# Gated DeltaNet layer: solving for the writes times the keys' reciprocal norms

## The chip, the cores and the metric

The kernel runs on one core of one Trainium2 chip. The time is the device time of one execution in microseconds (us); of several runs the median is given. A core has TensorE (PE, with its weight loads shown apart as PEld), VectorE (DVE), ScalarE (ACT), GpSimd (POOL) and SyncE (SP), which issues the DMAs of this kernel. Each engine works through its own queue in order and waits on semaphores that other engines raise.

## The reference

Two layers work on 1040 tokens (16 learned ones and 1024 given ones) of width 1024. Layer A is a gated DeltaNet with 8 heads of width 128; layer B is a latent attention that the change does not touch. Of layer A, what matters is this:

```python
k = l2_norm(k)                       # per token and head: k * rsqrt(sum(k*k) + EPS)
beta = sigmoid(b_raw)
g = -exp(a_log) * softplus(a_raw + dt_bias)
# per chunk, with gc = cumsum(g):
decay = exp(gc_i - gc_j) for j <= i
lower = strict_tril((k * beta) @ k.T * decay)
(I + lower) u = beta * v - (beta * k * exp(gc)) @ S      # solved for the writes u
o = (q * exp(gc)) @ S + tril(q @ k.T * decay) @ u
S = S * exp(gc_last) + (k * exp(gc_last - gc)).T @ u
```

The kernel works with chunks of 128 tokens (the recurrence is the same for any chunk length) and keeps the keys without their norm: with k_i = r_i * x_i, where x_i is the key before the norm and r_i its reciprocal norm, the norms are put into decays, key rows and betas.

## The kernel before

**Layout.** The tokens are one group of 16 (tile -1) and 8 tiles of 128. The projections give keys, queries and values with the channels on partitions (`kn`, `qT`, `vT`), by products of three f32r passes each (`mm3`, L93 to L95); a convolution of four taps follows on ACT and DVE (`conv_acts`, L396 to L402).

**Heads.** They go in four pairs (loop at L683). For a pair: values, queries, `query_prep`, `finish_inverses`, the scan over the 8 tiles (`scan_tile`), and then `prepare` of the next pair. The very first `prepare(0)` stands before the loop.

**`key_prep`** (L408), once for each head, on the keys of that head:
1. Key rows: `kn` is turned tile by tile on PE (L422), ACT squares each tile and sums it into `sk` (L423), `rsqrt` makes the reciprocal norms `rk` (a Newton step on DVE around ACT's logarithm and exponential, L177 to L182), `sc` = `rk` * `ekd` (L426), and the turned keys times `sc` are the rows `kd` (L428, two halves of four tiles) and `kdm` (L431). `ekd` is the decay up to the end of a tile.
2. Betas: `br` = beta * rk (L434), `nbeta` = -br (L435), `necb` = nbeta * egc (L437).
3. `br` is turned (L441, L442), copied to `brow`, `browm` (L443, L444) and sent to the scratch `beta_scr` (L445, L446), from where it comes back as `bb`.
4. Decays, for each half: POOL cuts `ghi` and `glo` into two tiles `gm` (L454, one buffer for each), PE sums them (L456), ACT takes the exponential into `att`, DVE multiplies by `rk` (L458), POOL zeroes what lies below the diagonal (L460). PE makes the products of keys with keys (L465), and DVE multiplies these by `att` into `U` (L466). The 16 first tokens have a small copy of all this (`attm`, `Um`, L471 to L480).
5. The 32x32 blocks on `U`'s diagonal go to `blk_in` (L486).

**`invert_blocks`** (L531) loads the blocks of both heads, multiplies by `bb` (L544) and inverts them by 31 steps of two DVE instructions (L549, L552). `finish_inverses` (L558) puts blocks together by small products and `nbeta` (L593, L608). **`scan_tile`** (L633) uses `necb`, `vb`, the inverse, `kd` and `att`: right side `r` (L638), writes `u` (L643), state `S` (L648), output `o` (L652, L653). **`value_rows`** (L670) turns `vT` into rows `vb`, `vbm`, times a scale per token (`natural`, L523, L528). **`query_prep`** multiplies `att` by the products of queries and keys (L509).

**Order.** The order on each engine is not the order of the text. A planner orders the instructions of the whole program before the launch, by program order, dependencies, buffers and durations that it assumes: between the instructions of one head's `key_prep` stand products of later projections and, from the second pair on, steps of the scan. Once planned, each engine's queue is fixed. The banks of PSUM with the tag `tr` (three) are shared by the turnings, the sums of decays and the products of keys. The `act` helper binds ACT's logarithm, exponential and Silu instructions into an order by table.

Of the kernel before, what the change touches and what calls it, by code (L numbers as in the profile page):

```python
# [16 lines left out]
F32 = mybir.dt.float32  # L17
# [3 lines left out]
ALU = mybir.AluOpType  # L21
PSUM = bass.MemoryType.PSUM

P = 128
D = 1024
NM = 16
T = 1024
L = NM + T
NT = T // P
# [3 lines left out]
EPS = 1e-6  # L33
# [88 lines left out]
def body(ctx: ExitStack, tc: tile.TileContext, I, out):  # L122
    nc = tc.nc
    V, A, G, TE, SY = nc.vector, nc.scalar, nc.gpsimd, nc.tensor, nc.sync
# [45 lines left out]
    def rsqrt(out_ap, in_ap, scale, bias):  # L170

        rows, *free = out_ap.shape
        w = int(np.prod(free))
        y, sh, t = (np2.tile([P, 32], F32, tag=x, name=nm(x))[0:rows, 0:w] for x in ("ny", "ns", "nt"))
        if len(free) == 2:
            y, sh, t = (x.rearrange("p (a b) -> p a b", b=free[1]) for x in (y, sh, t))
        V.tensor_scalar(out=sh, in0=in_ap, scalar1=-0.5 * scale, scalar2=-0.5 * bias, op0=ALU.mult, op1=ALU.add)  # L177
        act(y, sh, AF.Ln, scale=-2.0)
        act(y, y, AF.Exp, scale=-0.5)
        V.tensor_tensor(out=t, in0=y, in1=y, op=ALU.mult)  # L180
        V.tensor_tensor(out=t, in0=t, in1=sh, op=ALU.mult)
        V.scalar_tensor_tensor(out=out_ap, in0=t, scalar=1.5, in1=y, op0=ALU.add, op1=ALU.mult)  # L182
# [3 lines left out]
    with ExitStack() as la:  # L186
# [220 lines left out]

        def key_prep(h, kn, U):  # L408

            att, kd = ([kp.tile([P, 4, P], F32, tag=y, name=nm(y), bufs=6) for _ in range(2)] for y in ("att", "kd"))  # L410
            kdm = sp.tile([NM, P], F32, tag="kdm", name=nm("kdm"), bufs=3)
            hc = slice(h, h + 1)
            flat = lambda x: x.rearrange("p a b -> p (a b)")

            sc = sp.tile([P, NT + 1], F32, tag="ksc", name=nm("ksc"))
            for half, s4 in halves() + [(2, slice(NT, NT + 1))]:
                k, tiles = (P, range(s4.start, s4.stop)) if half < 2 else (NM, (-1,))
                ps = bank("tr", [P, 4, P])
                junk = sp.tile([P, P], BF16, tag="jk", name=nm("junk"), bufs=1)
                for j, t in enumerate(tiles):  # L420
                    a, b = tok(t)
                    TE.transpose(ps[0:k, j, :], kn[:, a:b], ident)  # L422
                    act(junk[0:k], ps[0:k, j, :], AF.Square, accum_out=sk[0:k, s4.start + j, hc])  # L423
                rk4, sc4 = flat(rk[0:k, s4, hc]), sc[0:k, s4]
                rsqrt(rk4, flat(sk[0:k, s4, hc]), 1.0, EPS)
                V.tensor_tensor(out=sc4, in0=rk4, in1=flat(ekd[0:k, s4, hc]), op=ALU.mult)  # L426
                if half < 2:
                    V.tensor_tensor(out=kd[half], in0=ps, in1=sc4[:, :, None].broadcast_to([P, 4, P]),  # L428
                                    op=ALU.mult)
                else:  # L430
                    V.tensor_scalar(out=kdm, in0=ps[0:k, 0, :], scalar1=sc4, scalar2=None, op0=ALU.mult)  # L431
            for rows, s in ((slice(0, P), slice(0, NT)), (slice(0, NM), slice(NT, NT + 1))):
                x = lambda y: flat(y[rows, s, hc])
                V.tensor_tensor(out=x(br), in0=x(beta), in1=x(rk), op=ALU.mult)  # L434
                V.tensor_scalar(out=x(nbeta), in0=x(br), scalar1=-1.0, scalar2=None, op0=ALU.mult)  # L435
                if s.start == 0:
                    V.tensor_tensor(out=x(necb), in0=x(nbeta), in1=x(egc), op=ALU.mult)  # L437
            ps = bank("tr", [P, 512])
            brow = sp.tile([H, P], F32, tag="brow", name=nm("brow"))
            browm = sp.tile([1, NM], F32, tag="browm", name=nm("browm"))  # L440
            TE.transpose(ps[0:NT, 0:P], flat(br[:, 0:NT, hc]), ident)  # L441
            TE.transpose(ps[0:1, P:P + NM], br[:NM, NT, hc], ident[:NM, :NM])  # L442
            V.tensor_copy(brow, ps[0:NT, 0:P])  # L443
            V.tensor_copy(browm, ps[0:1, P:P + NM])  # L444
            SY.dma_start(beta_scr[h, NM:].rearrange("(t p) -> t p", p=P), brow)  # L445
            SY.dma_start(beta_scr[hc, 0:NM], browm)  # L446

            for half, s4 in halves():
                ps = bank("tr", [P, 512])
                for i in range(2):  # L450
                    s2 = slice(s4.start + 2 * i, s4.start + 2 * i + 2)
                    gs = [bp.tile([P, 2, P], F32R, tag=f"g{y}", name=nm("gm")) for y in range(2)]
                    for y, gy in enumerate((ghi, glo)):
                        G.affine_select(out=gs[y], in_=gy[:, s2, hc].broadcast_to([P, 2, P]), compare_op=ALU.is_ge,  # L454
                                        fill=0.0, base=0, pattern=[[0, 2], [1, P]], channel_multiplier=-1)
                        TE.matmul(ps[:, 256 * i:256 * i + 256], after_r, flat(gs[y]), start=y == 0, stop=y == 1)  # L456
                act(flat(att[half]), ps, AF.Exp)
                V.tensor_tensor(out=att[half], in0=att[half], in1=rk[:, s4, hc].broadcast_to([P, 4, P]),  # L458
                                op=ALU.mult)
                G.affine_select(out=att[half], in_=att[half], compare_op=ALU.is_ge, fill=0.0, base=0,  # L460
                                pattern=[[0, 4], [1, P]], channel_multiplier=-1)
                ps = bank("tr", [P, 512])
                for j in range(4):
                    a, b = tok(4 * half + j)
                    TE.matmul(ps[:, P * j:P * j + P], kn[:, a:b], kn[:, a:b], start=True, stop=True)  # L465
                V.tensor_tensor(out=U[:, s4, :], in0=ps.rearrange("p (t i) -> p t i", i=P),  # L466
                                in1=att[half], op=ALU.mult)
            attm = sp.tile([NM, NM], F32, tag="attm", name=nm("attm"), bufs=3)
            Um = sp.tile([NM, NM], F32, tag="Um", name=nm("Um"))
            gmm = sp.tile([NM, NM], F32, tag="gmm", name=nm("gmm"))  # L470
            G.tensor_scalar(out=gmm, in0=upto[:NM, :NM], scalar1=g[:NM, NT, hc], scalar2=1.0,  # L471
                            op0=ALU.mult, op1=ALU.mult)
            ps = bank("tr", [P, 512])
            TE.matmul(ps[:NM, 0:NM], after[:NM, :NM], gmm, start=True, stop=True)
            act(attm, ps[:NM, 0:NM], AF.Exp)
            V.scalar_tensor_tensor(out=attm, in0=attm, scalar=rk[:NM, NT, hc], in1=upto[:NM, :NM],
                                   op0=ALU.mult, op1=ALU.mult)
            ps = bank("tr", [P, 512])
            TE.matmul(ps[:NM, 0:NM], kn[:, 0:NM], kn[:, 0:NM], start=True, stop=True)
            V.tensor_tensor(out=Um, in0=ps[:NM, 0:NM], in1=attm, op=ALU.mult)  # L480

            gi, hl = (h // 2) % 2, h % 2
            dst = blk_in[gi][33 * hl:33 * hl + 32].rearrange("(t q) j i -> q j t i", q=4)
            for q in range(4):
                r = slice(32 * q, 32 * q + 32)
                SY.dma_start(dst[q], U[r, :, r])  # L486
            SY.dma_start(blk_in[gi][33 * hl + 32, 0:NM, 0:NM], Um)
            return dict(att=att, attm=attm, kd=kd, kdm=kdm)
# [26 lines left out]
        def natural(src, scale, h, tag):  # L515

            x = kp.tile([P, NT, P], F32, tag=tag, name=nm(tag), bufs=3)
            for half, s4 in halves():
                ps = bank("tr", [P, 512])
                for j in range(4):  # L520
                    a, b = tok(4 * half + j)
                    TE.transpose(ps[:, P * j:P * j + P], src[:, a:b], ident)
                V.tensor_tensor(out=x[:, s4, :], in0=ps.rearrange("p (t i) -> p t i", i=P),  # L523
                                in1=scale[:, s4, h:h + 1].broadcast_to([P, 4, P]), op=ALU.mult)
            xm = sp.tile([NM, P], F32, tag=tag + "m", name=nm(tag + "m"))
            ps = bank("tr", [P, 512])
            TE.transpose(ps[:NM, 0:P], src[:, 0:NM], ident)
            V.tensor_scalar(out=xm, in0=ps[:NM, 0:P], scalar1=scale[:NM, NT, h:h + 1], scalar2=None, op0=ALU.mult)  # L528
            return x, xm
# [138 lines left out]
            hs[h]["qT"] = conv_acts(h * P, "qT", 2)  # L668

        def value_rows(h):  # L670
            hs[h]["vb"], hs[h]["vbm"] = natural(hs[h]["vT"], beta, h, "vb")

        def prepare(h0):
            U = kp.tile([P, 2, NT, P], F32, tag="U", name=nm("U"), bufs=2)
# [1008 lines left out]
```

## Time and profile before

| | |
|---|---|
| median of 3 runs | 1319.48 us (1317.81 to 1321.77) |
| the profiled execution | 1320.28 us |
| its span, first to last instruction | 1318.5 us |
| instructions | 25399 |
| mean granted TensorE clock | 0.988 |
| DVE, ACT, POOL busy | 902.6, 598.6, 319.3 us |
| moved by DMA | 68.19 MB read, 27.01 MB written |

Busy time is the time in which an engine works; waits for a semaphore are not in it. Matmuls overlap in PE's pipeline, so that a busy PE need not be at its peak. The layers lie one after the other: the work of `key_prep` starts at 57.9 us with the first turning of keys (L422) and the last head's products of keys with keys (L465) are issued at 445.0 us; the last write of the scan (L643) is at 563.2 us. "Idle before" is an engine's idle time ahead of an instruction, and the name behind the arrow is what ended it.

### The profile page before, as it was taken

How to read it: one execution, taken by the hardware profiler on the slowest of the kernel's cores; microseconds unless marked ns; L12 is line 12 of the kernel's file. 1: busy time of each engine (PE TensorE's matmuls, PEld its weight loads, DVE VectorE, ACT ScalarE, POOL GpSimd, SP SyncE). 2: the span in 40 equal slices, each digit the busy share in tenths (PEclk: the TensorE clock that was granted, in tenths of full speed). 3: DMA queues.
4: the chain of work that ended last, by engine and by line, in shares of the span. 5: the costliest groups of instructions: out<-in, count | busy, mean ns of one | idle time of the engine just before them, and what ended most of it. 6: DMA issues, size and time to landing. Idle time of an engine off the chain costs nothing.

```text
span 1318.5 us, 25399 instructions
## 1 busy us (share of the span) xinstructions
PE 1284.6 (97%) x9320; PEld 1199.6 (91%) x9320; DVE 902.6 (68%) x2534; ACT 598.6 (45%) x1764; POOL 319.3 (24%) x588
## 2 busy tenths in 40 slices
PE   6999999999999999999999999998999999998999
PEld 5889989989998999999999898887999999997888
DVE  7679789978986895663565655336878878777411
ACT  6543444344434431246522322127777777775200
POOL 3141121022111100040010113204544445447000
PEclk8999999999998999999999999998999999999999
DMA  5111112111111203165643014220101100015622
GB/s 198 33 34 47 52 29 55 41 45 38 59 49 31 54 32 98 58 219 159 183 128 99 25 33 130 81 90 17 51 25 50 44 29 26 21 39 168 202 90 79
DMA packets 95822, 96.85 MB, mean 73 GB/s; under 512 B 28526, under 2 KB 77614, under 8 KB 95698
## 3 DMA queue, kind: packets, MB, share of 16 engines
q1 hardware_dynamic: 95698, 95.23, 22.9%
q8 instruction: 73, 1.20, 0.4%
q14 instruction: 51, 0.42, 0.1%
HBM read 68.19 MB, written 27.01 MB: 72 GB/s over the span
## 4 chain that ended last, share of the span: by engine, by line
PE 82%; DVE 5%; ACT 3%; DMA 3%; issue 2%; POOL 2%; SPq 0%; DVEq 0%; ACTq 0%; POOLq 0%
PE mm L93 9%; PE mm L94 9%; PE mm L95 9%; PE sc L93 7%; PE sc L94 7%; PE sc L95 7%; PE bd L93 4%; PE bd L95 4%; PE bd L94 4%; PE pt L1502 2%; PE tr L508 1%; PE ch L640 1%; PE tr L500 1%; PE ch L650 1%; PE ch L636 1%
## 5 line engine op out<-in xcount | busy, mean ns | idle before, releaser
L93 PE MATMUL mm<-hT_hi,whi 128*128 128x384 f32 (+1 forms) x768 | 256.2, 334 | 4.7 <-ACT hT_hi L293 4.7
L94 PE MATMUL mm<-hT_lo,whi 128*128 128x384 f32 (+1 forms) x768 | 255.4, 333 | 0.1
L95 PE MATMUL mm<-hT_hi,wlo 128*128 128x384 f32 (+1 forms) x768 | 255.3, 332 | 0.0
L93 PEld LDWEIGHTS mm<-hT_hi,whi 128*128 128x128 f32 x768 | 146.6, 191 | 6.7 <-issue 5.8
L94 PEld LDWEIGHTS mm<-hT_lo,whi 128*128 128x128 f32 x768 | 146.6, 191 | 1.7 <-DVE hT_lo L294 0.6
L95 PEld LDWEIGHTS mm<-hT_hi,wlo 128*128 128x128 f32 x768 | 147.1, 192 | 1.1 <-issue 0.4
L100 POOL TENSOR_SCALAR whi<-raw 128x512 fp32r<-128x512 f32 x48 | 34.7, 739 | 164.9 <-PE mm L94 123.9
L113 DVE TENSOR_TENSOR pTl<-pt,pTh 128x256 fp32r<-128x256 f32 (+2 forms) x112 | 54.8, 494 | 13.4 <-ACT pTh L112 12.1
L93 PE MATMUL bd<-oTh,wf_hi 128*128 128x256 f32 (+1 forms) x192 | 60.7, 319 | 3.0 <-DVE xt L1624 3.0
L84 ACT ACTIVATE P<-P,mx 128x144 f32<-128x144 f32 (+3 forms) x64 | 50.6, 791 | 23.9 <-DVE mx L1460 18.0
L95 PE MATMUL bd<-oTh,wf_lo 128*128 128x256 f32 (+1 forms) x192 | 61.0, 318 | 0.0
L94 PE MATMUL bd<-oTl,wf_hi 128*128 128x256 f32 (+1 forms) x192 | 60.9, 318 | 0.0
L396 ACT COPY z<-mm 128x384 f32<-128x384 f32 (+1 forms) x72 | 32.0, 445 | 58.6 <-PE mm L95 57.7
L1624 DVE TENSOR_TENSOR xt<-bd,xt 128x256 f32<-128x256 f32 (+1 forms) x24 | 12.3, 514 | 67.4 <-PE bd L95 59.1
L1473 POOL TENSOR_SCALAR P<-P,sl 128x144 f32<-128x144 f32 (+3 forms) x64 | 52.9, 827 | 4.2
L112 ACT CAST pTh<-pt 128x256 fp32r<-128x256 f32 (+2 forms) x112 | 47.2, 428 | 13.0 <-PE pt L1502 6.1
L101 DVE TENSOR_TENSOR wlo<-raw,whi 128x512 fp32r<-128x512 f32 x64 | 46.8, 741 | 8.4 <-POOL whi L100 8.4
L400 DVE SCALAR_TENSOR_TENSOR kn<-z,pcol,kn 128x384 f32<-128x384 f32 (+1 forms) x72 | 42.1, 584 | 15.1 <-ACT kn L398 14.2
L93 PE MATMUL sc<-kn_hi,qn_hi 128*128 128x272 f32 (+3 forms) x160 | 48.3, 303 | 3.3 <-DVE mx L1460 2.7
L1502 PE MATMUL pt<-ident,P 128*128 128x128 f32 x288 | 47.7, 281 | 3.5 <-DVE pm L1494 1.9
L93 PE MATMUL sc<-h_hi,whi 128*128 128x512 f32 x128 | 50.7, 396 | 0.0
L94 PE MATMUL sc<-h_lo,whi 128*128 128x512 f32 x128 | 50.6, 395 | 0.0
(428 smaller groups left out, 4021.9 us busy)
## 6 DMA issues: line engine op xcount, KB each, us to landing
raw<-in_a_w_in SPq DMA_DIRECT2D x64, 256.0 KB
o_scr<-o SPq DMA_DIRECT2D x64, 64.0 KB
raw<-in_a_w_out SPq DMA_DIRECT2D x8, 512.0 KB
on<-o_scr SPq DMA_DIRECT2D x8, 512.0 KB
raw<-in_b_w_in SPq DMA_DIRECT2D x8, 512.0 KB
gb_scr<-z SPq DMA_DIRECT2D x8, 512.0 KB
gt<-gb_scr SPq DMA_DIRECT2D x32, 128.0 KB
ot_scr<-gt SPq DMA_DIRECT2D x32, 128.0 KB
```

The costliest lines, as they stand in the source:

```text
L84: i = A.activation(out_ap, in_ap, func, **kw)
L93: TE.matmul(ps, ahi, bhi, start=first, stop=False)
L94: TE.matmul(ps, ahi, blo, start=False, stop=False)
L95: TE.matmul(ps, alo, bhi, start=False, stop=last)
L100: eng.tensor_scalar(out=hi, in0=raw, scalar1=1.0, scalar2=1.0, op0=ALU.mult, op1=ALU.mult)
L101: V.tensor_tensor(out=lo, in0=raw, in1=hi, op=ALU.subtract)
L112: A.copy(hi, ps)
L113: V.tensor_tensor(out=lo, in0=ps, in1=hi, op=ALU.subtract)
L396: A.copy(z[:, 3 + a:3 + b], gemm_T(hi, lo, c))
L400: V.scalar_tensor_tensor(out=yc, in0=z[:, a + j:b + j], scalar=col("cw", 24 * j + m), in1=yc, op0=ALU.mult, op1=ALU.add)
L1473: G.tensor_scalar(out=Pm[:, 0:n], in0=Pm[:, 0:n], scalar1=s, scalar2=1.0, op0=ALU.mult, op1=ALU.mult)
L1502: TE.transpose(pt[:, kb, x * P:(x + 1) * P], Ps[x][0][:, y0 + kb * P:y0 + (kb + 1) * P], ident)
```

## The change

With w = r * u, the writes times the reciprocal norms, row i of the system is multiplied by r_i:

w_i + sum over j < i of (beta_i r_i^2) (x_i . x_j) decay_ij w_j = (beta_i r_i) v_i - (beta_i r_i^2) exp(gc_i) x_i S

The norms of the columns are then within w: `att` is the decay alone, the key rows are x * ekd, and state and output take them with w as before with u. So `nbeta` becomes -beta * rk^2, `beta_scr` gets beta * rk^2, and the values are scaled by `br` = beta * rk instead of `beta`.

```diff
         def key_prep(h, kn, U):
...
-            sc = sp.tile([P, NT + 1], F32, tag="ksc", name=nm("ksc"))
...
-                rk4, sc4 = flat(rk[0:k, s4, hc]), sc[0:k, s4]
-                rsqrt(rk4, flat(sk[0:k, s4, hc]), 1.0, EPS)
-                V.tensor_tensor(out=sc4, in0=rk4, in1=flat(ekd[0:k, s4, hc]), op=ALU.mult)
+                rsqrt(flat(rk[0:k, s4, hc]), flat(sk[0:k, s4, hc]), 1.0, EPS)
                 if half < 2:
-                    V.tensor_tensor(out=kd[half], in0=ps, in1=sc4[:, :, None].broadcast_to([P, 4, P]),
-                                    op=ALU.mult)
+                    V.tensor_tensor(out=kd[half], in0=ps, in1=ekd[:, s4, hc].broadcast_to([P, 4, P]), op=ALU.mult)
                 else:
-                    V.tensor_scalar(out=kdm, in0=ps[0:k, 0, :], scalar1=sc4, scalar2=None, op0=ALU.mult)
+                    V.tensor_scalar(out=kdm, in0=ps[0:k, 0, :], scalar1=ekd[0:k, NT, hc], scalar2=None, op0=ALU.mult)
...
                 V.tensor_tensor(out=x(br), in0=x(beta), in1=x(rk), op=ALU.mult)
-                V.tensor_scalar(out=x(nbeta), in0=x(br), scalar1=-1.0, scalar2=None, op0=ALU.mult)
+                V.scalar_tensor_tensor(out=x(nbeta), in0=x(br), scalar=-1.0, in1=x(rk), op0=ALU.mult, op1=ALU.mult)
...
-            TE.transpose(ps[0:NT, 0:P], flat(br[:, 0:NT, hc]), ident)
-            TE.transpose(ps[0:1, P:P + NM], br[:NM, NT, hc], ident[:NM, :NM])
-            V.tensor_copy(brow, ps[0:NT, 0:P])
-            V.tensor_copy(browm, ps[0:1, P:P + NM])
+            TE.transpose(ps[0:NT, 0:P], flat(nbeta[:, 0:NT, hc]), ident)
+            TE.transpose(ps[0:1, P:P + NM], nbeta[:NM, NT, hc], ident[:NM, :NM])
+            V.tensor_scalar(out=brow, in0=ps[0:NT, 0:P], scalar1=-1.0, scalar2=None, op0=ALU.mult)
+            V.tensor_scalar(out=browm, in0=ps[0:1, P:P + NM], scalar1=-1.0, scalar2=None, op0=ALU.mult)
...
                 act(flat(att[half]), ps, AF.Exp)
-                V.tensor_tensor(out=att[half], in0=att[half], in1=rk[:, s4, hc].broadcast_to([P, 4, P]),
-                                op=ALU.mult)
                 G.affine_select(out=att[half], in_=att[half], compare_op=ALU.is_ge, fill=0.0, base=0,
...
-            V.scalar_tensor_tensor(out=attm, in0=attm, scalar=rk[:NM, NT, hc], in1=upto[:NM, :NM],
-                                   op0=ALU.mult, op1=ALU.mult)
+            V.tensor_tensor(out=attm, in0=attm, in1=upto[:NM, :NM], op=ALU.mult)
...
         def value_rows(h):
-            hs[h]["vb"], hs[h]["vbm"] = natural(hs[h]["vT"], beta, h, "vb")
+            hs[h]["vb"], hs[h]["vbm"] = natural(hs[h]["vT"], br, h, "vb")
```

## The prediction

> **What bounds the kernel now.** I read the page first: who is busy, and what the chain that ended last is made of.
>
> ```profile
> PE 1284.6 (97%) x9320; PEld 1199.6 (91%) x9320; DVE 902.6 (68%) x2534; ACT 598.6 (45%) x1764; POOL 319.3 (24%) x588
> PE 82%; DVE 5%; ACT 3%; DMA 3%; issue 2%; POOL 2%; SPq 0%; DVEq 0%; ACTq 0%; POOLq 0%
> ```
>
> PE is busy in 97% of the span and carries 82% of the chain. But 68% for DVE is a mean over stages, and the change takes work from DVE in four of them: the preparation of the four pairs. So the second view is the busy time of the engines in these four stretches of 40 us (columns: stretch, length, then PE, PEld, DVE, ACT, POOL busy, granted clock, DMA).
>
> ```profile
> 60.00:100.00 40.00, 39.17 (x246) 33.67 (x246) 28.66 (x89) 20.84 (x71) 14.59 (x28) 1.00 0.15 41
> 180.00:220.00 40.00, 39.60 (x295) 37.48 (x295) 35.73 (x124) 17.69 (x66) 8.47 (x18) 1.00 0.20 52
> 300.00:340.00 40.00, 39.40 (x290) 37.12 (x289) 35.51 (x124) 17.63 (x66) 8.31 (x18) 1.00 0.19 50
> 430.00:470.00 40.00, 40.00 (x278) 38.47 (x278) 36.12 (x116) 17.30 (x55) 6.42 (x15) 1.00 0.19 55
> sum 160.00, PE 158.18 PEld 146.75 DVE 136.03 ACT 73.45 POOL 37.80; mean PE 39.54 PEld 36.69 DVE 34.01 ACT 18.36 POOL 9.45
> ```
>
> DVE is indeed near its limit there, 35.5 to 36.1 of 40 us in the later three, where the scan of one pair and the keys of the next share it. Yet PE is hardly idle: 160.00 - 158.18 = 1.8 us in all four. Whatever DVE is late with, PE mostly finds products of the next projections in its queue. What is left are short waits, so the third view is the waits of PE's weight loads from 60 to 560 us (total us, times, longest). Of these the change can touch:
>
> ```profile
> PEld tr L456 <- POOL gm L454: 5.0, 17, 0.7
> PEld ch L640 <- DVE r L638: 1.6, 8, 0.3
> PEld ch L620 <- DVE Nm L575: 1.5, 2, 0.8
> PEld tr L500 <- DVE M L552: 1.3, 5, 0.3
> PEld tr L441 <- DVE br L434: 0.7, 2, 0.5
> ```
>
> One group waits for POOL's cuts of the decays (5.0 us), three for DVE (1.6 + 1.5 + 1.3 = 4.4 us), and 0.7 us is the wait of the turning of `br`. Together 10.1 us, or 0.8% of the time, and far from all of it goes.
>
> **The change part by part.** The costs on DVE, by the groups of instructions (count | busy us, mean ns of one):
>
> ```profile
> L458 DVE TENSOR_TENSOR att<-att,rk 128x512 f32<-128x512 f32 x16 | 11.9, 746 | 4.3 <-ACT att L84 4.1
> L428 DVE TENSOR_TENSOR kd<-tr,ksc 128x512 f32<-128x512 f32 x16 | 10.8, 677 | 0.0
> L523 DVE TENSOR_TENSOR vb<-tr,beta 128x512 f32<-128x512 f32 x16 | 10.8, 679 | 1.3 <-PE tr L522 1.3
> L426 DVE TENSOR_TENSOR ksc<-rk,ekd 128x4 f32<-128x4 f32 (+1 forms) x24 | 3.2, 153 | 0.1
> L182 DVE SCALAR_TENSOR_TENSOR rk<-nt,ny 128x4 f32<-128x4 f32 (+1 forms) x24 | 3.1, 151 | 0.2
> L435 DVE TENSOR_SCALAR nbeta<-br 128x8 f32<-128x8 f32 (+1 forms) x16 | 2.1, 144 | 0.0
> L443 DVE COPY brow<-tr 8x128 f32<-8x128 f32 x8 | 2.2, 271 | 1.1 <-PE tr L442 1.0
> L431 DVE TENSOR_SCALAR kdm<-tr,ksc 16x128 f32<-16x128 f32 x8 | 2.6, 331 | 0.0
> ```
>
> - Removed: the multiplication of the decays by `rk` (L458), 16 x 746 ns = 11.9 us, and `ksc` (L426), 3.2 us in 24 instructions. `attm` (16 x 16) loses an operand, which I take as nothing. Sum 15.1 us.
> - Added: `nbeta` becomes the form of L182 with two tensors, 16 x (151 - 144) ns = 0.1 us. `brow` becomes a multiplication from PSUM; the nearest row is L431, 16 partitions by 128, so 8 x (331 - 271) ns = 0.5 us. `browm` is of the same kind but 16 elements long; I put it between nothing and the same 0.5 us, and take nothing. Sum 0.6 us.
> - Unchanged: `vb` reads `br` instead of `beta`, the same shape and steps; no new wait in effect, since `br` is made in the same queue during the preparation and `vb` follows it there. The DMAs are as before, and each queue keeps its number of transfers.
> - `kd` and `kdm` read `ekd` directly, with a step of 8 elements from tile to tile, where `ksc` was compact. `vb` (L523) already reads its scale with that step: 679 ns against 677. I take nothing; 16 x 2 ns is no cost.
>
> [...]
>
> So DVE gets 15.1 - 0.6 = 14.5 us back, 11% of its 136.0 us in the four stretches. None of that is on PE's path by itself; it counts only through the waits above. Three terms:
>
> *Cuts of the decays (L456 waiting for L454).* PE waits for POOL, not for DVE. But POOL's cuts get slow beside DVE. A place where this shows (the timeline; start us, us):
>
> ```profile
> 87.36 0.69 DVE L458 TENSOR_TENSOR att<-att,rk 128x512 f32<-128x512 f32 x1 [1.34 <-ACT att L84]
> 87.56 0.77 POOL L454 TENSOR_SCALAR_AFFINE_SELECT gm<-ghi 128x256 fp32r<-128x256 f32 x1 [0.38 <-PE tr L456]
> 88.28 0.40 POOL L454 TENSOR_SCALAR_AFFINE_SELECT gm<-glo 128x256 fp32r<-128x256 f32 x1
> 88.38 0.38 PE L456 MATMUL tr<-gm,after_r 128*128 128x256 f32 x1 [0.28 <-POOL gm L454]
> ```
>
> The cut that starts during L458 takes 0.77 us, the next one 0.40, and PE then stands idle for it. All cuts together:
>
> ```profile
> L454 POOL TENSOR_SCALAR_AFFINE_SELECT gm<-ghi 128x256 fp32r<-128x256 f32 x32 | 15.0, 469 | 60.4 <-PE tr L456 60.0
> L454 POOL TENSOR_SCALAR_AFFINE_SELECT gm<-glo 128x256 fp32r<-128x256 f32 x32 | 14.7, 461 | 3.8 <-PE tr L456 3.7
> ```
>
> Against 0.40 us each the 64 cuts lose 29.7 - 64 x 0.40 = 4.1 us to such meetings. L458 is only one of the instructions that they can meet (the convolution's L400 is another, and stays), so I take a third: 1.4 us on POOL, and since PE waited 17 times for 64 cuts, I choose to credit PE with half of it, -0.7 us. Bounds: -4.1 (all of it was L458) and 0.
>
> [...]
>
> *Waits for DVE (4.4 us).* With 11% less to do there, I let them shrink by 11%: -0.5 us. Bounds: -4.4 and 0.
>
> *The turning of the betas.* L441 now reads `nbeta` instead of `br`, so one more DVE instruction stands before it. Behind L441 in PE's queue is the whole of PE's work. For the first and the last of the eight heads:
>
> ```profile
> 68.33 0.15 DVE L434 TENSOR_TENSOR br<-beta,rk 128x8 f32<-128x8 f32 x1
> 68.55 0.28 PE L441 MATMUL tr<-ident,br 128*8 128x128 f32 x1
> 69.28 0.15 DVE L435 TENSOR_SCALAR nbeta<-br 128x8 f32<-128x8 f32 x1
> 437.51 0.15 DVE L434 TENSOR_TENSOR br<-beta,rk 128x8 f32<-128x8 f32 x1
> 438.21 0.27 PE L441 MATMUL tr<-ident,br 128*8 128x128 f32 x1
> 439.36 0.15 DVE L435 TENSOR_SCALAR nbeta<-br 128x8 f32<-128x8 f32 x1
> ```
>
> Between `br` and `nbeta` DVE did other things, among them `kd` and `kdm` (677 and 331 ns), which needed `rk`. In the changed kernel these need only the turned keys, so they can go before the norms, and `nbeta` can follow `br` directly: one instruction of 0.15 us more. If PE waits for it eight times as long as for `br`, that is 8 x 0.15 = 1.2 us; where L441 is put later in PE's queue it is nothing. I take the middle, +0.6 us. Bounds: -0.7 (the present wait goes) and the price of the second rival.
>
> Sum: -0.7 - 0.5 + 0.6 = -0.6 us on the profiled execution's 1320.28 us (span 1318.5 and 1.8 around it), so 1319.7 us. That execution was 0.8 us above the median 1319.48, so against the median 1318.9 us. I round the forecast to **1318.7 us**. The 14.5 us off DVE are nearly all hidden under the products on PE (L93 to L95). If that cover were gone, they would be worth up to 14.5 us; PE's idle 1.8 us says that it is not.
>
> **The rivals.**
>
> *DVE's relief reaches PE (faster).* For it: DVE at 36 of 40 us beside a PE that waits in small pieces; against it: PE's 1.8 us of idle. All five groups of waits above gone would be 10.1 us; two thirds of that, with the shorter hold of the `tr` banks (`kd` no longer waits for the norm), is -6.7 us: about **1312.8 us**. Beyond 10.1 us nothing in the waits can pay.
>
> *The turning waits in PE's queue (slower).* If L441 keeps its place and `nbeta` its own, PE stands until `nbeta` is ready: 69.28 + 0.15 - 68.55 = 0.9 us for the first head, 439.36 + 0.15 - 438.21 = 1.3 us for the last. At the smaller price for eight heads this is 8 x 0.9 = 7.2 us, less the two gains: +6.0, about **1325.5 us**. It decides from the point where more than 0.5 us of DVE work lies between the two instructions. For it: in the last pairs steps of the scan go between them. Against: the order is planned anew, with the dependency known.
>
> *A new order.* Fewer and shorter instructions shift everything that is planned after 58 us, layer B's products too. What the order is worth is seen in the pairs of heads, which do the same work in different orders. The first turning of squared queries (L500) of each pair in the chain:
>
> ```profile
> 120.62 2.01 PE tr L500 x18
> ...
> 240.97 2.01 PE tr L500 x18
> ...
> 360.37 2.01 PE tr L500 x18
> ...
> 482.52 2.01 PE tr L500 x18
> ```
>
> The three periods are 120.35, 119.40 and 122.15 us. So order (and clock) make 1 to 3 us a pair, of either sign: over four pairs I allow 5 us up or down, **1314** or **1324 us**.
>
> **How the numbers follow.** About 0.3%, 4 us, is what a measurement of this kernel can tell from no change. Chances: forecast within 4 us 0.52, relief reaches PE 0.20, turning waits 0.12, a new order that is better 0.09, one that is worse 0.07. So faster 0.29, same 0.52, slower 0.19. The range reaches to both large rivals with a little of their spread: 1310.5 to 1325.5 us; below it would need all 10.1 us, above it the larger price of the turning.
>
> **What would show it.** Right: DVE's busy time about 14.5 us lower, no L458 and L426, `kd` still near 677 ns, cuts that are slow only beside L400, PE's idle in the preparation still about 2 us, the waits for `r` and `Nm` nearly as long. Wrong: L441 among PE's waits with several us (second rival), or a span that falls by more than the waits listed here, which would mean that PE's busy time hid stalls that I did not count; or layer B's part changed, which would be the order.

## The result, and the profile after

The changed kernel takes 1328.52 us (median of 11 executions, 1319.94 to 1336.07) against 1321.30 us for the kernel before (11 executions beside them, 1317.81 to 1325.51): a ratio of 1.0045 [1.0027, 1.0063] (the brackets hold the 95% interval). It is slower by 0.3 to 0.6%, where practically no change (-0.6 us) was forecast.

The profiled execution of the changed kernel took 1323.27 us (span 1321.6, 25352 instructions), which is at the low end of its own spread. A second profile of the same kernel (called after_again below; 1332.85 us, span 1331.1) is the slowest of its own six executions. Both are used, since what differs between them turned out to be the answer.

The page of the changed kernel, busy time and chain:

```profile
PE 1285.0 (97%) x9320; PEld 1202.0 (91%) x9320; DVE 894.3 (68%) x2494; ACT 597.3 (45%) x1764; POOL 316.7 (24%) x588
PE 81%; DVE 5%; ACT 4%; issue 3%; DMA 3%; POOL 2%; SPq 0%; DVEq 0%; ACTq 0%; POOLq 0%
```

DVE did lose work, PE is as busy as before, and its 1285.0 us are within 0.4 us of the 1284.6 before. By this view nothing has happened. The same holds for the four stretches of the preparation (sum over the same 160 us as in the prediction):

```profile
sum 160.00, PE 158.94 PEld 148.22 DVE 130.18 ACT 75.78 POOL 38.30; mean PE 39.73 PEld 37.05 DVE 32.54 ACT 18.95 POOL 9.57
```

PE's idle time there is 160.00 - 158.94 = 1.1 us, against 1.8 before. And the waits of PE's weight loads from 58 to 570 us that the prediction had listed (total us, times, longest):

```profile
PEld tr L454 <- POOL gm L452: 4.0, 17, 0.5
PEld ch L635 <- DVE r L633: 2.1, 10, 0.4
PEld ch L615 <- DVE Nm L570: 1.8, 2, 1.3
PEld tr L495 <- DVE M L547: 0.5, 2, 0.2
PEld tr L439 <- DVE br L432: 0.2, 1, 0.2
```

Against the same stretch of the kernel before (58 to 570 us, where the wait for `r` is 1.8), the first shrank by 1.0 us, the second and third grew by 0.3 each, the last two shrank by 0.8 and 0.5. None of this is 7 us, and the turning of `nbeta` (L439, formerly L441) is a wait of only 0.2 us. So the loss is not among the waits. It shows in a column that the prediction read past: the granted clock of TensorE, last but two in the view by stretches. Layer A as one stretch, first in the kernel before, then in the first and the second profile of the changed one:

```profile
58.00:565.00 507.00, 504.07 (x4109) 469.64 (x4108) 405.89 (x1188) 204.50 (x637) 84.26 (x162) 0.99 0.17 48
```

```profile
58.00:565.00 507.00, 503.82 (x4106) 471.55 (x4104) 394.92 (x1145) 203.07 (x637) 83.07 (x162) 0.98 0.16 48
```

```profile
58.00:565.00 507.00, 504.05 (x4040) 472.85 (x4039) 389.45 (x1125) 200.66 (x627) 82.88 (x162) 0.96 0.17 48
```

PE is busy for 504 of 507 us in all three, but at 0.99, 0.98 and 0.96 of its clock: it fits 4109, 4106 and 4040 products into the same stretch. A second profile of the kernel before (before_again below) has 0.98 and 4100 products there, so that the first profile of the changed kernel lies within what the kernel before does: its span is 1321.6 us at a clock of 0.989, that of before_again 1321.7 us at 0.988. The second profile of the changed kernel is the one that stands out. The scan's last write, in the kernel before and in the second profile of the changed one (timeline):

```profile
563.25 0.29 DVE L643 COPY u<-ch 128x128 f32<-128x128 f32 x1 [0.15 <-PE ch L641]
```

```profile
573.35 0.29 DVE L638 COPY u<-ch 128x128 f32<-128x128 f32 x1 [0.15 <-PE ch L636]
```

10.1 of the 12.6 us between these two spans (1331.1 - 1318.5) are lost by the end of the scan.

### The profile page after: what moved, and what is told of

The parts are those of the page before. It is cut to its first block, busy times and chain, and to the rows that moved or that the text cites. A ratio compares the mean times of both kernels' runs of the same rounds, so it can differ in the third digit from the quotient of the medians.

```text
span 1321.6 us, 25352 instructions
## 1 busy us (share of the span) xinstructions
PE 1285.0 (97%) x9320; PEld 1202.0 (91%) x9320; DVE 894.3 (68%) x2494; ACT 597.3 (45%) x1764; POOL 316.7 (24%) x588
## 4 chain that ended last, share of the span: by engine, by line
PE 81%; DVE 5%; ACT 4%; issue 3%; DMA 3%; POOL 2%; SPq 0%; DVEq 0%; ACTq 0%; POOLq 0%
PE mm L93 9%; PE mm L94 8%; PE mm L95 8%; PE sc L93 7%; PE sc L94 7%; PE sc L95 7%; PE bd L93 4%; PE bd L94 4%; PE bd L95 4%; PE pt L1497 2%; PE tr L503 1%; PE ch L635 1%; PE tr L495 1%; PE ch L645 1%; PE ch L631 1%
## 5 line engine op out<-in xcount | busy, mean ns | idle before, releaser
L113 DVE TENSOR_TENSOR pTl<-pt,pTh 128x256 fp32r<-128x256 f32 (+2 forms) x112 | 54.7, 494 | 13.5 <-ACT pTh L112 12.1
L95 PE MATMUL sc<-h_hi,wlo 128*128 128x512 f32 x128 | 50.5, 394 | 0.0
```

Of the source, the lines that this page charges most:

```text
L95: TE.matmul(ps, alo, bhi, start=False, stop=last)
L113: V.tensor_tensor(out=lo, in0=ps, in1=hi, op=ALU.subtract)
```

## The experiments

All eleven were timed in five rounds beside the kernel before. "Clock" is the mean granted clock over the executions of a run, with its range; "loss" is the mean of span x (1 - clock), the time's worth of clock that was not granted.

| kernel | median us (range; executions) | ratio to before [95%] | clock | loss us |
|---|---|---|---|---|
| before_again | 1322.26 (1318.47 to 1326.10; 12) | 0.9997 [0.9983, 1.0011] | 0.988 (0.984 to 0.992) | 15.3 |
| after_again | 1331.52 (1328.62 to 1332.85; 6) | 1.0060 [1.0041, 1.0080] | 0.979 (0.977 to 0.983) | 27.9 |
| betas_only | 1323.28 (1319.91 to 1325.04; 12) | 1.0000 [0.9986, 1.0013] | 0.990 (0.988 to 0.992) | 13.5 |
| no_decay_scale | 1327.12 (1322.74 to 1333.90; 12) | 1.0042 [1.0025, 1.0059] | 0.983 (0.978 to 0.985) | 23.0 |
| after_ones | 1324.91 (1319.65 to 1329.57; 12) | 1.0009 [0.9991, 1.0027] | 0.986 (0.982 to 0.991) | 18.6 |
| after_wide | 1330.20 (1326.31 to 1337.70; 6) | 1.0067 [1.0041, 1.0092] | 0.987 (0.981 to 0.991) | 18.0 |
| before_wide | 1319.34 (1316.96 to 1329.03; 12) | 0.9984 [0.9967, 1.0001] | 0.993 (0.983 to 0.996) | 9.7 |
| before_bf16 | 1305.70 (1302.10 to 1310.78; 6) | 0.9872 [0.9844, 0.9900] | 0.992 (0.988 to 0.995) | 11.1 |
| after_bf16 | 1309.15 (1305.34 to 1317.77; 6) | 0.9909 [0.9878, 0.9940] | 0.989 (0.982 to 0.992) | 14.8 |
| before_twice | 1318.16 (1317.56 to 1320.28; 12) | 0.9972 [0.9959, 0.9984] | 0.991 (0.989 to 0.994) | 11.4 |
| after_twice | 1337.53 (1323.71 to 1340.47; 6) | 1.0113 [1.0089, 1.0136] | 0.978 (0.973 to 0.991) | 29.6 |

### Both kernels again: before_again, after_again

The two kernels, unchanged.

> The kernel before itself, timed beside its own runs, so that the granted clock of each of its runs is known (of the changed kernel's 11 runs it is: 0.977 to 0.989, and the product of span and clock is 1300 to 1307 us in all of them). Clock theory (the change leaves the work of TensorE alone and only moves which stretches meet a lowered clock): the product of span and clock is 1300 to 1306 us, and the clock stays at 0.985 or above in most runs. Stall theory (the changed order makes TensorE wait): the product is 1297 to 1302 us, some 5 us under that of the changed kernel run beside it, at the same clocks.

> The changed kernel again, on the same chip as the others. Clock theory: product of span and clock within 2 us of that of the kernel before, and all of the difference in time (about 6 us) in the clock. Stall theory: product 4 to 6 us higher, clock the same.

The difference is there again, 0.6%, and with it a lower clock, 0.979 against 0.988. Span x clock, an estimate of the time that the same work would take at full clock, has a mean of 1301.3 us in after_again against 1305.3 in the kernel before beside it. It is lower by 4.0 us: the stall theory, which wanted it 4 to 6 us higher, is refuted, and the clock theory, which wanted it within 2 us, is nearer but not met, since the loss rose by more (12.2 us) than the time (8.3 us). Over all executions whose clock is on record the kernel before has a mean of 1322.6 us at a mean loss of 15.7 us (91 executions), the changed one 1329.3 us at 24.5 us (17 executions).

### One part alone: betas_only, no_decay_scale

The kernel before with only the new betas, turned from `nbeta`:

```diff
-                V.tensor_scalar(out=x(nbeta), in0=x(br), scalar1=-1.0, scalar2=None, op0=ALU.mult)
+                V.scalar_tensor_tensor(out=x(nbeta), in0=x(br), scalar=-1.0, in1=x(rk), op0=ALU.mult, op1=ALU.mult)
...
-            TE.transpose(ps[0:NT, 0:P], flat(br[:, 0:NT, hc]), ident)
+            TE.transpose(ps[0:NT, 0:P], flat(nbeta[:, 0:NT, hc]), ident)
...
-            V.tensor_copy(brow, ps[0:NT, 0:P])
+            V.tensor_scalar(out=brow, in0=ps[0:NT, 0:P], scalar1=-1.0, scalar2=None, op0=ALU.mult)
```

> The kernel before with only the betas of the change: nbeta is -beta * rk * rk, and nbeta is turned instead of br. The decays and key rows keep their norms, so the output is another one. If the turning of the later nbeta holds TensorE (the slower rival of the prediction): 3 to 7 us slower than before at the same clock, and nbeta among the waits of TensorE. Clock theory: within 2 us of before in the product of span and clock, the time where the clock puts it.

The kernel before without the multiplication of the decays:

```diff
-                V.tensor_tensor(out=x(br), in0=x(beta), in1=x(rk), op=ALU.mult)
+                V.scalar_tensor_tensor(out=x(br), in0=x(beta), scalar=1.0 / 64, in1=x(rk), op0=ALU.mult, op1=ALU.mult)
...
-                V.tensor_tensor(out=att[half], in0=att[half], in1=rk[:, s4, hc].broadcast_to([P, 4, P]),
-                                op=ALU.mult)
```

> The kernel before with only the multiplication of the decays by rk left out (and that of attm); br is scaled by 1/64 in the same instruction, so that the numbers stay small; the output is another one. DVE has 11.9 us less to do. If the missing instruction gives a worse order (stall theory): slower than before by 3 to 6 us in the product of span and clock. If the relief reaches TensorE: faster by 2 to 6 us. Clock theory: product within 2 us of before; the time moves only with the clock.

The new betas cost nothing that shows: 1.0000 [0.9986, 1.0013]. The kernel without the multiplication (`br` also has another form in it, and `attm` loses an operand) is slower by about what the whole change is, 1.0042 [1.0025, 1.0059], at a clock of 0.983. Its span x clock is 1303.1 us, not above the 1305.3 of the kernel before, so it does not lose by work or waits of PE. What less work on DVE can do is to move PE's products in time. That it is the removal as such which does the harm is not shown by this: the nudges below move the loss as well, and they only add work.

### The work put back: after_ones

The changed kernel with an equal instruction where L458 stood, a multiplication by ones:

```diff
+                V.tensor_tensor(out=att[half], in0=att[half], in1=ones[:, 0:4, None].broadcast_to([P, 4, P]),
+                                op=ALU.mult)
```

> The changed kernel with a multiplication of the decays by ones where the multiplication by rk stood: DVE gets the 11.9 us back, the output is that of the reference. If what costs is the missing instruction and the order that is planned without it: the clock's loss (span times one minus clock) falls from the changed kernel's 23 to 28 us to about 15 us, the product of span and clock rises to about 1305 us, and the time is that of before, 1320 to 1324 us. If another part of the change (key rows, betas, value scale) makes the loss: 1327 to 1332 us as the changed kernel.

1.0009 [0.9991, 1.0027]: with 16 useless instructions more the changed kernel is no longer measurably slower than the kernel before, and the loss is down from 24.5 to 18.6 us. It is not back at the 15 us that were expected, and 1324.91 us lies just above the expected 1320 to 1324.

### Where the clock falls

The traces show the granted clock as steps: it is 1 or 0.5, and each lowered stretch is 3.41 us long or a multiple of that (in the kernel before 3.41 us from 138.53, 6.83 from 903.11, 10.24 from 401.35). Their starts lie on a grid of 10.24 / 3 = 3.413 us, whose offset to the span's first instruction differs from trace to trace (the lowered window behind the second head's sums starts at 139.38 us in the first profile of the changed kernel and at 139.74 in the second, 0.36 us or a tenth of a step apart); a window is the time between two lines of it. In the 13 traces layer A's lowered stretches begin behind one of two places: the sums of the squared queries in `query_prep` (18 products with a column of ones for each head, L500, after the change L495), or the small products of `finish_inverses`. PE is nearly always busy there as the profile counts it (3.41 of 3.41 us with the sums below, 2.67 of 3.41 with the inverses), but each product streams few columns, one in the sums and 64 in the products L606 and L611 of the kernel before.

The first pair in the kernel before, cut at the grid's lines (stretch, length, then PE, PEld, DVE, ACT, POOL busy, clock):

```profile
118.05:121.46 3.41, 3.41 (x24) 3.14 (x22) 3.41 (x9) 0.43 (x1) 0.86 (x1) 1.00 0.26 79
121.46:124.88 3.42, 3.42 (x31) 3.27 (x31) 3.39 (x9) 2.24 (x5) 1.88 (x2) 1.00 0.00 0
135.12:138.53 3.41, 3.41 (x28) 3.14 (x28) 2.08 (x7) 1.62 (x3) 1.28 (x2) 1.00 0.00 0
138.53:141.94 3.41, 3.41 (x19) 3.15 (x17) 3.41 (x12) 0.23 (x1) 0.10 (x1) 0.50 0.25 79
```

and what stands there (timeline of PE):

```profile
120.56 2.08 PE L500 MATMUL tr<-ones,sq 128*16 128x1 f32 x18
122.50 2.03 PE L508 MATMUL tr<-qT,kn 128*128 128x128 f32 x16
...
136.28 2.08 PE L500 MATMUL tr<-ones,sq 128*16 128x1 f32 x18
138.22 3.48 PE L508 MATMUL tr<-qT,kn 128*128 128x128 f32 x16
```

The first head's sums (120.56 to 122.50) straddle the line at 121.46, and the next window keeps the full clock. The second head's sums (136.28 to 138.22) lie whole between 135.12 and 138.53, and the following window has 0.50: the same 16 products behind them take 3.48 us instead of 2.03. PE shows 3.41 of 3.41 us busy in every row, so busy time says nothing about it. In the second profile of the changed kernel the first head's sums also lie whole in a window (timeline, then the stretches):

```profile
119.69 2.08 PE L495 MATMUL tr<-ones,sq 128*16 128x1 f32 x18
121.63 2.83 PE L503 MATMUL tr<-qT,kn 128*128 128x128 f32 x16
```

```profile
119.26:122.67 3.41, 3.41 (x30) 3.14 (x30) 3.38 (x9) 1.69 (x4) 2.68 (x2) 1.00 0.00 0
122.67:126.08 3.41, 3.41 (x17) 3.15 (x17) 3.41 (x10) 0.66 (x3) 0.00 (x1) 0.50 0.25 79
136.33:139.74 3.41, 3.41 (x30) 3.14 (x29) 2.05 (x7) 1.62 (x3) 1.26 (x2) 1.00 0.00 0
139.74:143.15 3.41, 3.41 (x18) 3.15 (x17) 3.41 (x11) 0.52 (x1) 0.10 (x1) 0.50 0.27 77
```

I counted all undivided groups of 18 one-column sums in the nine traces that have them (both profiles of each kernel, betas_only, no_decay_scale, after_ones, and the two with a doubled instruction), each against the grid of its own trace:

| place of the group | groups | next window lowered |
|---|---|---|
| across a line of the grid | 35 | 0 |
| within one window, the last sum starts 0.18 us or more before its end | 29 | 29 |
| within one window, the last sum starts 0.10 and 0.12 us before its end | 2 | 0 |

By kernel, lowered behind queries: 1 and 2 of 8 heads in the two profiles of the kernel before, 4 and 6 of 8 in the two of the changed one. But betas_only has 4 at a mean loss of 13.5 us, no_decay_scale 2 at 23.0, after_ones 4 at 18.6, before_twice 2 at 11.4 and after_twice 4 at 29.6: the number in one profiled execution does not follow the mean loss of its kernel. A lowered window also feeds the next: in the chain of the second profile the two heads of a pair stand 17.20 us apart where the first was lowered, and in the chain of the kernel before (prediction, 240.97, and below) 15.72 us where it was not.

```profile
256.69 2.01 PE tr L500 x18
```

```profile
119.76 2.01 PE tr L495 x18
136.96 2.01 PE tr L495 x18
```

So a lowered window here costs 17.20 - 15.72 = 1.5 us. And 15.72 us are 4.61 steps of the grid, 17.20 are 5.04: the second head then falls on nearly the same place in its window as the first, and is lowered too. In the first three pairs of the nine traces the first head was lowered eight times, and each time the second was too; where the first was not lowered, the second was in 12 of 19 cases.

The small products of `finish_inverses` are the second place. In the second profile of the changed kernel (timeline of PE):

```profile
280.43 0.39 PE L615 MATMUL ch<-vbm,Nm 16*16 16x128 f32 x2 [1.07 <-DVE Nm L570]
...
281.07 1.90 PE L601 MATMUL fin<-T,U 64*64 64x64 f32 x32
282.89 1.06 PE L617 MATMUL ch<-um,kdm 16*128 16x128 f32 x4
...
286.09 3.31 PE L606 MATMUL fin<-U,T 64*64 64x64 f32 x32
```

```profile
279.69:283.10 3.41, 2.67 (x36) 2.26 (x37) 1.33 (x5) 2.57 (x7) 0.10 (x1) 1.00 0.35 111
283.10:293.34 10.24, 10.24 (x62) 9.01 (x62) 3.67 (x11) 4.73 (x20) 0.52 (x1) 0.50 0.01 3
```

In the kernel before, the same two groups of 32 products came 4.2 us apart with other products between them, and the clock stayed up (timeline, then the stretches between lines of the grid):

```profile
284.56 1.90 PE L606 MATMUL fin<-T,U 64*64 64x64 f32 x32
...
288.74 1.90 PE L611 MATMUL fin<-U,T 64*64 64x64 f32 x32
```

```profile
283.91:287.32 3.41, 3.41 (x42) 2.96 (x42) 2.14 (x7) 1.23 (x7) 0.00 (x0) 1.00 0.01 2
287.32:290.74 3.42, 3.35 (x42) 2.69 (x40) 2.95 (x10) 0.67 (x2) 1.58 (x4) 1.00 0.02 5
```

There too each group lies whole within one window, so that alone does not lower the clock. In after_again the wait for `Nm` (1.07 us idle) and the first group of 64x64 products fell into one window; three lowered windows followed, with the second group, 3.31 us instead of 1.90, inside them. For this place I have cases, not a count like the one above.

### The sums made wider: after_wide, before_wide

Each sum streams 56 equal columns instead of one:

```diff
-                TE.matmul(ps[0:b - a, s:s + 1], sq[:, a:b], one, start=True, stop=True)
+                TE.matmul(ps[0:b - a, 56 * s:56 * s + 56], sq[:, a:b], ones[:, 0:56], start=True, stop=True)
```

> The changed kernel with the sums of squares of the queries (18 products of one column each for a head, 2 us in which TensorE streams next to nothing) made 56 columns wide, of which one is read; the same number of products. Clock theory (a lowered clock follows stretches in which few columns are streamed): no lowered clock behind these stretches any more, the loss falls from 23 to 28 us to 12 to 18 us, the product stays at 1301 to 1306 us, time 1314 to 1322 us. If the lowered clock has nothing to do with these stretches: loss and time as the changed kernel, 1327 to 1332 us, or longer by the wider products.

> The same widening in the kernel before. Clock theory: its loss falls from 15.5 us to 8 to 13 us (the lowered clock after the queries goes, that at the inverses and in layer B stays), time 1314 to 1321 us; then the changed kernel so widened is no slower than this one by more than 3 us. Otherwise 1321 to 1325 us as before.

Behind the queries the mechanism held: no window behind the queries is lowered in either profile, though 15 of their 16 groups lie within one window, with the last sum 0.24 us or more before its end; of one-column groups in that place all were lowered. A group takes 2.19 us instead of 2.08, so it is not the time of the group that counts, but how much it streams, 56 columns a product against one. The clock rose in both kernels (0.993 against 0.988, 0.987 against 0.979). The time is a hit for the kernel before only as a tendency (0.9984 [0.9967, 1.0001]) and a miss for the changed kernel: 1.0067 [1.0041, 1.0092]. After_ones had 1324.9 us at a loss of 18.6; after_wide, at 18.0, took 5 us more. And it is 10.9 us slower than before_wide, where at most 3 were expected. A part of this is a wait that came with the widening: a product behind the sums (L507, in the kernel before L512) now waits until DVE has read them into `epsq` (waits of PE in after_wide, then in before_wide; the other f32 kernels have none of it).

```profile
PE tr L507 <- DVE epsq L497: 2.5, 4, 1.1
PE tr L512 <- DVE epsq L502: 2.0, 3, 1.0
```

That is 2.5 of the 5 us, and the longer groups take 8 x 0.11 = 0.9 us. Where the rest lies is open.

### The sums made shorter: before_bf16, after_bf16

Squares and the column of ones in bf16:

```diff
+    one_b = ctile("one_b", [P, 2], BF16)
+    V.tensor_copy(one_b, ones[:, 0:2])
...
-            sq = kp.tile([P, L], F32, tag="vT", name=nm("sq"), bufs=1)
+            sq = kp.tile([P, L], BF16, tag="vT", name=nm("sq"), bufs=1)
...
-                TE.matmul(ps[0:b - a, s:s + 1], sq[:, a:b], one, start=True, stop=True)
+                TE.matmul(ps[0:b - a, s:s + 1], sq[:, a:b], one_b[:, 0:1], start=True, stop=True)
```

> The kernel before with the squares of the queries and the column of ones in bf16: one pass of TensorE for each sum instead of two, 9 instead of 18 products a head, so that the stretch of one-column products lasts 1 us instead of 2. The sums only enter the small constant of the output's norm. By the work alone: 8 heads x 1 us = 8 us less, about 1315 us, if the clock's loss stays at 15.5 us. Clock theory: the shorter stretch brings fewer lowered windows behind the queries, the loss falls to 8 to 12 us and the time to 1309 to 1313 us. If the clock has nothing to do with the stretch: loss 15 to 16 us.

> The same in the changed kernel. By the work alone: 1329 - 8 = 1321 us with a loss of 23 to 28 us. Clock theory: the windows behind the queries (five of twelve lowered windows in the slower profile of the changed kernel's layer A) go, the loss falls to 10 to 18 us, the time to 1310 to 1317 us.

This is the one version that beats both kernels: 0.9872 [0.9844, 0.9900] in the kernel before, 0.9909 [0.9878, 0.9940] in the changed one. A head's sums are 9 products and not 18 (page and timeline of before_bf16):

```profile
PE 1274.6 (97%) x9248; PEld 1188.2 (91%) x9248; DVE 903.4 (69%) x2535; ACT 598.7 (46%) x1764; POOL 313.1 (24%) x588
```

```profile
120.97 0.45 PE L502 MATMUL tr<-one_b,sq 128*16 128x1 bf16 x9
121.28 2.03 PE L510 MATMUL tr<-qT,kn 128*128 128x128 f32 x16
```

0.45 us instead of 2.08 makes 8 x 1.63 = 13.0 us of PE's own time, where the expectation had 8 (the sum of PE's busy time fell by 10.0 us, 1284.6 to 1274.6); the means are 1322.6 - 1306.3 = 16.3 us apart, and a loss of clock that is 15.7 - 11.1 = 4.6 us smaller is enough for the rest. So most of the gain is work, not clock, and both times came out below what was expected (1305.7 us against 1309 to 1313, 1309.15 against 1310 to 1317). No head's sums are followed by a lowered window in either trace; what is lowered in layer A there lies behind the inverses.

### A nudge: before_twice, after_twice

One small DVE instruction is issued twice, `ksc` (L426) in the kernel before, `nbeta` in the changed one. That changes the order, and nothing of PE's work:

```diff
+                V.tensor_tensor(out=sc4, in0=rk4, in1=flat(ekd[0:k, s4, hc]), op=ALU.mult)
```

```diff
+                V.scalar_tensor_tensor(out=x(nbeta), in0=x(br), scalar=-1.0, in1=x(rk), op0=ALU.mult, op1=ALU.mult)
```

> The kernel before with the small product ksc issued twice: 24 more DVE instructions of 0.15 us, 3.7 us in all, no change of meaning or of TensorE's work. If a new order alone moves the clock's loss: the loss differs from 15.5 us by more than 3 us in either direction and the time goes with it by 0.7 of that, at the same time at full clock. If what the change does (less work on DVE) makes the loss: loss 14 to 17 us and time 1321 to 1325 us.

> The changed kernel with nbeta issued twice: 16 more DVE instructions of 0.15 us, 2.4 us in all, no change of meaning or of TensorE's work. If the clock's loss of 24.5 us belongs to the one order that the planner made of the change: the loss moves by more than 3 us (likely down, towards the 10 to 19 us of most other orders), the time follows by 0.7 of it, and what is left at full clock stays at 1311 to 1314 us. If the change itself brings the loss (less work for DVE): loss 22 to 27 us, time 1327 to 1332 us.

More work made the kernel before faster, 0.9972 [0.9959, 0.9984], at a loss of 11.4 us. The changed kernel got slower still, 1.0113 [1.0089, 1.0136], at 29.6 us; I had expected its loss to fall, so the direction of a nudge can't be told ahead. Its six executions went from 1323.71 us at a clock of 0.991 to 1340.47 us at 0.973: one program, 17 us apart.

## Why the prediction was wrong

**The step that failed** is the reading of PE's busy time: "Yet PE is hardly idle: 160.00 - 158.18 = 1.8 us", from which followed that nothing but the waits, 10.1 us in all, could move. Busy time counts a product at half clock as fully as one at full clock: in the kernel before the window from 138.53 us, at 0.50, and the one from 135.12, at 1.00, both have 3.41 of 3.41 us. The sum had no term for the granted clock at all, and took over the 0.988 of the kernel before. The missing term is 24.5 - 15.7 = 8.8 us of clock. Over the 192 executions, within one kernel, 1 us more of loss went with 0.65 us more of time; by that the term is 0.65 x 8.8 = 5.7 of the 6.7 us between the two means (1329.3 - 1322.6). If a lost microsecond of clock costs a whole one, which the clock's three digits (0.001 is 1.3 us) would blur, it is all of them. At equal clocks the change is then worth something from -2.1 to +1.0 us; -0.6 was forecast. (The stated 1318.7 us is 0.2 under the prediction's own sum of 1318.9; that decides nothing.)

**A new order** was the right rival with the wrong size and cause. "So order (and clock) make 1 to 3 us a pair" had the clock in brackets. The longest of the three periods, 122.15 us, holds the stretch from 401.35 us where this trace was lowered for 10.24 us; the shortest, 119.40, holds none. The middle one, 120.35, holds one lowered window, at 138.53. It was largely a view of the clock, read as one of order. I allowed 1324 us at a chance of 0.07; the medians are 1328.5 and 1331.5.

**The relief of DVE** went nowhere, as forecast. Its busy time fell by 902.6 - 894.3 = 8.3 us rather than 14.5: by 11.0 in the stretch from 58 to 565 us, while other groups and the rest of the program gave some back. Two new forms were dearer than I took them, `nbeta` and `attm` (groups of the changed kernel):

```profile
L433 DVE SCALAR_TENSOR_TENSOR nbeta<-br,rk 128x8 f32<-128x8 f32 (+1 forms) x16 | 3.4, 216 | 0.1
L472 DVE TENSOR_TENSOR attm<-attm,upto 16x16 f32<-16x16 f32 x8 | 2.3, 288 | 1.9 <-ACT attm L84 1.9
L441 DVE TENSOR_SCALAR brow<-tr 8x128 f32<-8x128 f32 x8 | 2.2, 272 | 1.2 <-PE tr L440 1.2
L427 DVE TENSOR_TENSOR kd<-tr,ekd 128x512 f32<-128x512 f32 x16 | 10.9, 683 | 0.0
```

`nbeta` takes 216 ns and not 151, 1.3 us in all instead of 0.1. `attm`, taken as nothing, takes 288 ns where the form before took 221. Both are dear only beside POOL: the five small `nbeta` (16x1) and the two `attm` that overlap cuts or other elementwise work of POOL take 247 to 749 ns, all others 142 to 179. That is the meeting which the prediction priced for POOL's cuts alone; here it slows DVE. `brow` is 272 against 271, where I had added 0.5 us. `kd` with the step of 8 elements is 683 against 677 ns, so nothing, as taken.

**The cuts of the decays** were right: POOL's 64 cuts fell from 29.7 us to 28.5, by 1.2 (1.4 forecast), and PE's wait for them by 1.0 (0.7 forecast).

```profile
L452 POOL TENSOR_SCALAR_AFFINE_SELECT gm<-glo 128x256 fp32r<-128x256 f32 x32 | 15.0, 468 | 1.0 <-PE tr L454 0.8
L452 POOL TENSOR_SCALAR_AFFINE_SELECT gm<-ghi 128x256 fp32r<-128x256 f32 x32 | 13.5, 423 | 49.0 <-PE tr L454 48.9
```

**The waits for DVE** were to shrink by 0.5 us; `r`, `Nm` and `M` together are 4.4 us, against 4.6 in the same stretch (58 to 570 us) of the kernel before. **The turning** was to cost 0.6 us, and its wait went from 0.7 to 0.2. betas_only speaks against the rival built on it, which was priced at +6 us and measured nothing, 1.0000 [0.9986, 1.0013]. "Layer B's part changed, which would be the order" was listed as a sign of error; in the second profile of the changed kernel most of the loss is in layer A instead (507 x 0.04 = 20 us of 1331.1 x 0.021 = 28).

**What stays open.** That the one-column sums, whole within a window, lower the next one is shown by the count and by both edits of the sums. Why the mean loss of the changed kernel is 8.8 us higher is not shown. That its order puts more such stretches whole into windows is only an argument: the profiles of these two kernels fit it (1 and 2 heads against 4 and 6), betas_only and no_decay_scale do not, and as the grid's offset differs from execution to execution, the order alone does not decide where a group falls. The clock of the other executions is only known as a mean. No threshold in columns was found that holds for all windows. Of after_wide's 5 us about a third is unexplained.

## What to carry to other kernels

Read the granted clock beside busy time before forecasting: TensorE, 97% busy here in every page, still lost 0.7 to 2.2% of the span to its clock, in layer A behind short stretches of one-column sums or of the small products of the inverses. An edit elsewhere that only shifts these stretches moved the mean by 4.3 us one way (before_twice) and 5.7 the other (after_twice). A difference of half a per cent between two planned orders should be checked by a nudge that does nothing, such as a doubled small instruction, before it is credited to the edit. What paid in these runs was not to tune the order but to shorten a stretch that streams little, as the sums in bf16 do.

## What the runs showed of the hardware

The granted clock went to 0.50 in steps of 3.41 us, on a grid whose lines lie elsewhere from execution to execution: one is at 139.38 us in the first profile of the changed kernel and at 139.74 in the second. PE was busy, as the profile counts it, for 3.41 of 3.41 us in the window ahead of a lowered one (119.26 to 122.67 us in after_again), and 121.63 - 119.69 = 1.94 us of one-column sums in it were enough; of the groups that lay so, with the last sum 0.18 us or more before the window's end, 29 of 29 were followed by a lowered window, and of those across a line none of 35. The loss came to 9.7 to 29.6 us on average, 0.7 to 2.2% of the span.
